# Eight pairs of input tiles of the feed-forward output multiplied by seven block products, three by plain products

## The chip, the cores and the metric

The kernel runs on one core of a Trainium2 chip. The metric is device time in microseconds of one execution, lower is better. Engine names: PE is TensorE (PEld its weight loads), DVE is VectorE, ACT is ScalarE, POOL is GpSimd, SP is SyncE, which here only issues DMAs. ACT issues some DMAs as well.

## The reference

One layer with 1024 tokens and 1024 features. Four mixer branches are gated and merged, then comes a gated feed-forward, then a gated embedding, then a norm. The change is in the second line of the feed-forward; the code of the gates and of the feed-forward input shares a helper with it.

```python
h = rmsnorm(x, g_mix[i])
...
merged = sum(jax.nn.sigmoid(h @ w_merge_gate[i, br]) * (branches[br] @ w_branch[i, br])
             for br in range(N_BRANCH))
x = x + merged @ w_out[i]
h2 = rmsnorm(x, g_ffn[i])
f_gate, f_up = jnp.split(h2 @ w_ffn_in[i], 2, axis=-1)
x = x + (jax.nn.silu(f_gate) * f_up) @ w_ffn_out[i]      # hidden width 2816 = 22 tiles of 128
h3 = rmsnorm(x, g_ple[i])
x = x + jax.nn.sigmoid(h3 @ w_ple_gate[i]) * (p[i].astype(x.dtype) @ w_ple_proj[i])
return rmsnorm(x, g_final)
```

## The kernel before

Features lie on partitions and tokens along the rows, so an activation tile is 128 features by 1024 tokens (512 KB). Every product is computed in three parts to keep the precision of float32: a value is split in a rounded high part (a cast on ACT) and the rest (a subtraction on DVE), the helper `split`, L110 and L111; the matmuls then add high x high, high x low and low x high.

Gates and feed-forward input use `pair` (L537): two output tiles and all eight input tiles at once, as a two by two block product with seven products where eight would be plain. Its weights come in two loads of 512 KB, `ra` and `rb`. `sums` makes the seven weight operands out of them: three are blocks as they come, four are sums or differences on POOL (L548 to L557). `product` splits one such operand and runs 12 matmuls of 128x128 by 512 columns on it. Products 0, 2 and 4 add up in one PSUM bank, `u`, and between them ACT copies its value out (L576 after product 0, L583 after product 2, L588 after product 4); product 2 can't start before the copy after product 0 is done. The seven activation operands (`OPS`) are made once before a stage by `operands`, seven tiles for each of the four pairs of input tiles, 28 tiles in all.

The feed-forward input is 11 steps of two pairs, `fg` (gate half) and `fu` (up half); a step takes its number `j` from its first hidden tile, 0, 2, ... 20. DVE scales and multiplies the blocks (L703 to L709), ACT applies Silu (L706), and ACT's queue stores the two hidden tiles of a step to DRAM in four DMAs of 256 KB (L714).

The feed-forward output, L716 to L767, reads the 22 hidden tiles back (`load_parts`, L167), splits each once and runs plain three-part products in two chunks of hidden tiles, 14 and 8, and two groups of four output tiles. `x2` is the running sum of the layer. After the last chunk `n3.add` makes the next norm's operands (L191, L192) and its sum of squares (L196, L200) of each output tile; in the second group one output tile at a time is finished, so that this work lies beside the products of the next tile. The stage behind it (`pg`, `pq`) needs all eight tiles.

The order of each engine's instructions is fixed when the program is built. Each engine, and each queue that issues DMAs, takes its instructions in that order: what waits keeps everything behind it waiting. Buffers come from pools: 38 of 512 KB for `T`, 8 for `M`, 3 for raw weights `W`, 4 pairs for split weights `WP`. A load into a buffer waits until its last reader is done.

Of the kernel before, what the change touches and what calls it, by code (L numbers as in the profile page):

```python
# [13 lines left out]
P = 128  # L14
# [10 lines left out]
CHUNKS = ((0, 14), (14, 22))  # L25
# [13 lines left out]
def mixers_kernel(ctx, tc, xT, pT, vec, mask, sgu_ln, sgu_wT, sgu_b, w_in, w_tok, w_gate, w_br, w_out,  # L39
                  w_fi, w_fo, w_pg, w_pp, outT):  # L40
# [25 lines left out]
    def M(name, w=S, dt=F32):  # L66
        return mp.tile([P, w], dt, tag="m", name=name, padded_shape=[P, S], bufs=8)
# [4 lines left out]
    def WS(name):  # L72
        return wp.tile([P, 512], F32, tag="sw", name=name, bufs=2)
# [278 lines left out]
    def qk(ct):  # L352

        qs, kd = [], []
        kl = None
        for nm, i in (("q", 6 + ct), ("k", 8 + ct)):
            ps = proj_tile(i)
            t = T(f"{nm}{ct}")
            if nm == "q":
                nc.vector.scalar_tensor_tensor(t, ps, -(64.0 ** -0.5), rs, ALU.mult, ALU.mult)  # L360
                for h in range(2):
                    a, b = slice(h * 64, h * 64 + 64), slice(64 - h * 64, 128 - h * 64)
                    d = M(f"qs{ct}{h}", S, F32R)
                    nc.scalar.copy(d[a, :], t[a, :])
                    nc.vector.tensor_sub(d[b, :], t[a, :], d[a, :].bitcast(F32))
                    qs.append(d)
            else:
                nc.vector.tensor_mul(t, ps, rs)
                kl = M(f"kl{ct}", S, F32R)
                for h in range(2):  # L370
                    a, b = slice(h * 64, h * 64 + 64), slice(64 - h * 64, 128 - h * 64)
                    d = M(f"kd{ct}{h}", S, F32R)
# [60 lines left out]
    sgc = M("sgc", 6 * P).rearrange("p (g c) -> p g c", c=P)  # L433
# [77 lines left out]
    def operand(name, p, i, src):  # L511

        t = T(f"{name}o{p}i{i}", F32R)
        split(t[:, :512], t[:, 512:], src)
        OPS[p][i] = t

    def operands(name, i, xa, xb, have=()):

        a1, a2, b1, b2 = xa[:, :512], xa[:, 512:], xb[:, :512], xb[:, 512:]
        t12, t34 = M(f"{name}t12i{i}"), M(f"{name}t34i{i}")  # L520
        t1, t2, t3, t4 = t12[:, :512], t12[:, 512:], t34[:, :512], t34[:, 512:]
        if 0 not in have:
            operand(name, 0, i, a1)
        nc.vector.tensor_sub(t1, a2, a1)
        operand(name, 1, i, t1)
        nc.vector.tensor_sub(t2, b2, t1)
        operand(name, 2, i, t2)
        if 3 not in have:
            operand(name, 3, i, b1)
        nc.vector.tensor_sub(t3, b2, a2)  # L530
        operand(name, 4, i, t3)
        if 5 not in have:
            operand(name, 5, i, b2)
        nc.vector.tensor_sub(t4, b1, t2)
        operand(name, 6, i, t4)

    def pair(name, wa, wb):  # L537

        ra = W(f"{name}ra")
        nc.sync.dma_start(ra, wa)  # L540
        rb = W(f"{name}rb")
        nc.sync.dma_start(rb, wb)
        a1, a2, b1, b2 = ra[:, :512], ra[:, 512:], rb[:, :512], rb[:, 512:]

        def sums():
            yield a1
# [12 lines left out]
            yield b2

        def product(p, src, ps, first):
            hi, lo = WP(f"{name}p{p}")
            split(hi, lo, src)
            for i in range(4):
                x = OPS[p][i]
                wh, wl = hi[:, i * P:(i + 1) * P], lo[:, i * P:(i + 1) * P]
                for n, (w, c) in enumerate(((wh, 0), (wh, 512), (wl, 0))):
                    nc.tensor.matmul(ps, w, x[:, c:c + 512], start=(first and i == 0 and n == 0),  # L568
                                     stop=(i == 3 and n == 2), skip_group_check=not first)
# [95 lines left out]
    for m0 in (0, 1, 2, 3, 4, 5, 6):  # L665
# [58 lines left out]
    for ci, (k0, k1) in enumerate(CHUNKS):
        fs = {}
        for grp in range(2):
            last = ci == 1 and grp == 1
            if not last:
                ps = [[A(f"fo{ci}{grp}{mm}{h}") for h in range(2)] for mm in range(4)]
                for k in range(k0, k1):  # L730
                    if grp == 0:
                        fs[k] = load_parts(f"f{k}", fd[k])
                    if k % 2 == 0:
                        raw = W(f"fow{grp}{k}")
                        nc.sync.dma_start(raw, w_fo[:, (grp * NJ + k) * 512:(grp * NJ + k + 2) * 512])
                        w = w_parts(f"fow{grp}{k}", raw, S)
                    for mm in range(4):
                        for i, (n, p) in enumerate(((0, 0), (0, 1), (1, 0))):
                            for h in range(2):
                                nc.tensor.matmul(ps[mm][h], w[k % 2 * 4 + mm][n], fs[k].part(p, h * 512, h * 512 + 512),  # L740
                                                 start=(k == k0 and i == 0), stop=(k == k1 - 1 and i == 2))
            if ci == 1 and not last:
                for k in range(2):
                    raw = W(f"pp{k}r")
                    nc.sync.dma_start(raw, pT[k * P:(k + 1) * P, :])
                    pp.append(parts(f"pp{k}", raw))
            for mm in range(4):
                m = 4 * grp + mm
                if last:
                    pm = [A(f"fo{ci}{grp}{mm}{h}") for h in range(2)]  # L750
                    w = []
                    n = (k1 - k0) * P
                    for c in range(0, n, S):
                        e = min(c + S, n)
                        raw = W(f"fol{m}{c}", e - c)
                        nc.sync.dma_start(raw, w_fo[:, (NJ + k0) * 512 + mm * n + c:(NJ + k0) * 512 + mm * n + e])
                        w += w_parts(f"fol{m}{c}", raw, e - c)
                    for k in range(k0, k1):
                        for h in range(2):
                            mm_k(pm[h], w[k - k0], fs[k], k == k0, k == k1 - 1, ((h * 512, h * 512 + 512),), h * 512)  # L760
                else:
                    pm = ps[mm]
                for h in range(2):
                    t = x2[m][:, h * 512:h * 512 + 512]
                    nc.vector.tensor_add(t, pm[h], t)  # L765
                if ci == 1:
                    n3.add(m, x2[m])  # L767
# [101 lines left out]
def _layout(i):  # L869
# [15 lines left out]
    def taps(w):  # L885
# [22 lines left out]
    wo = a["w_ffn_out"][0].reshape(NJ, P, 2, 4, P)  # L908
    k1 = CHUNKS[1][0]
    out["w_fo"] = np.concatenate([t.reshape(P, -1) for t in (  # L910
        wo[:, :, 0].transpose(1, 0, 2, 3), wo[:k1, :, 1].transpose(1, 0, 2, 3), wo[k1:, :, 1].transpose(1, 2, 0, 3))], 1)
# [20 lines left out]
```

## Time and profile before

| | us |
|---|---|
| median of 3 runs (1609.58 to 1611.53) | 1611.34 |
| the profiled execution's own time | 1612.55 |
| its span in the trace | 1610.8 |
| PE busy | 1588.8 (99%) |
| DVE busy | 1031.6 (64%) |
| ACT busy | 640.0 (40%) |
| POOL busy | 215.1 (13%) |
| feed-forward input, steps 2 to 20 (847.7 to 1232.7) | 385.0 |
| feed-forward output (1232.7 to 1472.3) | 239.6 |

Durations are read from the profiled execution, whose own time is 1.21 us above the median. A matmul's record overlaps the next one, so a rate is read from the distance of starts and not from a record's length; the same holds for DVE, where one record of 0.69 us starts 0.60 us after the last.

### The profile page before, as it was taken

Reading aid. Unit: us, or ns where it says so; the run is one execution under the profiler, and the core shown is the slowest. Engines: PE = TensorE matmul, PEld = TensorE weight load, DVE = VectorE, ACT = ScalarE, POOL = GpSimd, SP = SyncE. Lnnn points to the kernel's source line nnn. Section 1 sums busy time; section 2 is a strip of 40 time slices with the busy share of each in tenths; the row PEclk is TensorE's granted clock in tenths of the full one; section 3 lists DMA queues with packets and bytes.
Section 4 is the critical chain, followed back from the end, with each engine's and each line's share of the span. In section 5 each row is a group of like instructions: output and inputs, shape, how many; then the busy total and the mean of one; then the engine's idle time right before and its main releaser. Section 6 shows DMA issues by size and latency. Waiting matters only on the chain.

```text
span 1610.8 us, 19722 instructions
## 1 busy us (share of the span) xinstructions
PE 1588.8 (99%) x7626; PEld 1309.6 (81%) x7626; DVE 1031.6 (64%) x1506; ACT 640.0 (40%) x1068; POOL 215.1 (13%) x158
## 2 busy tenths in 40 slices
PE   9999999999999999999999999999999999999997
PEld 7976788778888888888888888888888888888886
DVE  6988785755567667686776666666666431354456
ACT  6335554233434334354553333433334411133334
POOL 0000000112222222200122322223220000000000
PEclk9999999999999999999999999999999999999998
DMA  6110233121212212213442222222225531211214
GB/s 223 53 40 14 70 129 108 66 79 47 92 53 72 66 52 73 66 59 135 140 176 79 85 79 87 94 82 79 81 89 172 207 92 53 68 41 46 66 47 141
DMA packets 46718, 140.93 MB, mean 87 GB/s; under 512 B 5280, under 2 KB 8608, under 8 KB 46624
## 3 DMA queue, kind: packets, MB, share of 16 engines
q1 hardware_dynamic: 39024, 125.98, 23.8%
q10 hardware_dynamic: 7600, 13.69, 2.3%
q8 instruction: 60, 0.98, 0.3%
q14 instruction: 34, 0.28, 0.1%
HBM read 115.53 MB, written 24.12 MB: 87 GB/s over the span
## 4 chain that ended last, share of the span: by engine, by line
PE 88%; DVE 8%; DMA 1%; ACT 1%; issue 0%; ACTq 0%; SPq 0%; DVEq 0%
PE fo L740 12%; PE pj L151 10%; PE wo L151 5%; PE br L151 5%; PE pg L151 5%; PE fo L151 3%; PE po L413 1%; PE sc L394 1%; PE pq L151 1%; PE ptp L407 1%; PE sc L393 1%; PE sp L317 1%; PE sp L315 1%; PE fu20u L568 1%; PE gt63u L568 1%; PE gt43u L568 1%
## 5 line engine op out<-in xcount | busy, mean ns | idle before, releaser
L330 DVE SCALAR_TENSOR_TENSOR cacc<-cy,vs,cacc 128x1023 f32<-128x1023 f32 (+29 forms) x60 | 75.7, 1263 | 0.5
L408 ACT COPY pt<-ptp 128x512 f32<-128x512 f32 (+3 forms) x48 | 21.8, 481 | 35.5 <-PE ptp L407 35.5
L814 DVE TENSOR_TENSOR pt<-pg,n3r 128x768 f32<-128x768 f32 (+1 forms) x16 | 11.0, 689 | 29.7 <-PE pg L151 29.7
L398 DVE CUSTOM_DVE_ANT_0 pr<-sc,maskt 128x128 f32<-128x128 f32 (+7 forms) x32 | 24.1, 753 | 9.1 <-PE sc L394 8.8
L151 PE MATMUL pj<-n1p,w1h 128*128 128x512 f32 x96 | 27.7, 408 | 1.4 <-ACT n1p L191 1.4
L765 DVE TENSOR_TENSOR x<-fo,x 128x512 f32<-128x512 f32 x32 | 20.9, 687 | 12.5 <-PE fo L151 11.3
L400 ACT ACTIVATE pr<-pr,nm 128x128 f32<-128x128 f32 (+7 forms) x32 | 24.9, 779 | 5.5 <-DVE nm L398 5.3
L438 POOL TENSOR_SCALAR_AFFINE_SELECT sgc<-sgc 128x512 f32<-128x512 f32 x1 | 1.3, 1322 | 168.8 <-DMA sgc<-in_sgu_wT 168.8
L151 PEld LDWEIGHTS pj<-n1p,w1h 128*128 128x128 f32 x96 | 18.7, 196 | 6.2 <-ACT n1p L191 2.2
L413 PE MATMUL po<-pt,vt 128*64 128x128 f32 x288 | 22.7, 279 | 0.2
L407 PE MATMUL ptp<-ident,pr 128*128 128x128 f32 x144 | 22.2, 276 | 0.0
L413 PEld LDWEIGHTS po<-pt,vt 128*64 128x64 f32 x288 | 16.9, 136 | 5.8 <-issue 2.8
L394 PE MATMUL sc<-kl,qs 64*128 64x512 f32 (+3 forms) x48 | 21.0, 438 | 0.0
L815 ACT ACTIVATE pt<-pt 128x768 f32<-128x768 f32 (+1 forms) x16 | 10.1, 630 | 26.3 <-DVE pt L814 26.3
L682 DVE TENSOR_TENSOR xr<-wo,xr 128x512 f32<-128x512 f32 x16 | 11.0, 688 | 14.8 <-PE wo L151 14.7
L407 PEld LDWEIGHTS ptp<-ident,pr 128*128 128x128 f32 x144 | 16.6, 140 | 3.1 <-ACT rb L418 1.0
L393 PE MATMUL sc<-kd,qs 128*128 128x512 f32 (+3 forms) x48 | 18.7, 390 | 0.1
L548 POOL TENSOR_TENSOR gt00s<-gt00rb 128x512 f32<-128x512 f32 x1 | 1.3, 1292 | 131.1 <-DMA gt00rb<-in_w_gate 131.1
L683 ACT ACTIVATE x1g<-xr,vs 128x512 f32<-128x512 f32 x16 | 11.6, 724 | 18.0 <-DVE xr L682 18.0
L394 PEld LDWEIGHTS sc<-kl,qs 64*128 64x128 f32 x48 | 8.8, 183 | 10.0 <-issue 8.6
L822 ACT ACTIVATE pt<-x 128x768 f32<-128x768 f32 (+1 forms) x13 | 8.4, 647 | 19.0 <-DVE x L818 19.0
L151 PE MATMUL pj<-n1p,w1l 128*128 128x512 f32 x48 | 15.3, 398 | 0.0
(4222 smaller groups left out, 5306.7 us busy)
## 6 DMA issues: line engine op xcount, KB each, us to landing
fow<-in_w_fo SPq DMA_DIRECT2D x18, 512.0 KB, 3.8
xg<-in_xT SPq DMA_DIRECT2D x8, 512.0 KB, 4.2
xr<-in_xT SPq DMA_DIRECT2D x8, 512.0 KB, 5.1
x1d<-xr SPq DMA_DIRECT2D x8, 512.0 KB, 2.9
x<-x1d SPq DMA_DIRECT2D x8, 512.0 KB, 5.8
x<-in_xT SPq DMA_DIRECT2D x7, 512.0 KB, 7.5
vpr<-in_w_tok SPq DMA_DIRECT2D x4, 512.0 KB, 4.8
spr<-in_w_tok SPq DMA_DIRECT2D x4, 512.0 KB, 3.6
```

Of the source, the lines that this page charges most:

```text
L151: nc.tensor.matmul(ps[:, c - off:e - off], w[n], act.part(p, c, e), start=(first and i == 0), stop=(last and i == 2))
L330: nc.vector.scalar_tensor_tensor(acc[:, d:], y[:, :S - d], wj, acc[:, d:], ALU.mult, ALU.add)
L393: nc.tensor.matmul(sc[:, c:c + n], q, kd[h][:, c:c + n], start=True, stop=False)
L394: nc.tensor.matmul(sc[:, c:c + n], q[a, :], kl[a, c:c + n], start=False, stop=True)
L398: nc.vector.tensor_tensor_reduce(out=pr[:, :L], in0=sc[:, :L], in1=maskt[:, S - L:], scale=1.0, scalar=NEG, op0=ALU.add, op1=ALU.min, accu ...
L400: nc.scalar.activation(pr[:, :L], pr[:, :L], AF.Exp, bias=nm, scale=-1.0, accum_out=ls)
L407: nc.tensor.transpose(pa[:, j * P:(j + 1) * P], pr[:, c + j * P:c + (j + 1) * P], ident)
L408: nc.scalar.copy(pt[:, c:c + n], pa[:, :n])
L413: nc.tensor.matmul(po[h * 64:h * 64 + 64, :P], vtok[j // 4][:, hc:hc + 64], pts[h][:, j * P:(j + 1) * P], start=(j == 0), stop=(j == b))
L568: nc.tensor.matmul(ps, w, x[:, c:c + 512], start=(first and i == 0 and n == 0), stop=(i == 3 and n == 2), skip_group_check=not first)
L740: nc.tensor.matmul(ps[mm][h], w[k % 2 * 4 + mm][n], fs[k].part(p, h * 512, h * 512 + 512), start=(k == k0 and i == 0), stop=(k == k1 - 1 a ...
L765: nc.vector.tensor_add(t, pm[h], t)
```

## The change

The output of the feed-forward now takes pairs of hidden tiles 0 to 3 and 4 to 7 (two chunks of four pairs, 16 hidden tiles) through `pair`, four pairs of output tiles for each chunk, and hidden pairs 8, 9 and 10 through plain products (`single`). The order is single 8, chunk 0, single 9, chunk 1, single 10. `n3.add` follows each output tile of single 10.

What is stored to DRAM is no longer the hidden tile but the split operands: seven tiles of 512 KB for a pair in a chunk, four for a single one. They are made one step later than their blocks, one after each block of the following step (`next(steps)`), and stored by ACT's queue. The reads back (`load_hidden`) have no split behind them. The operand tiles come from `M`, and so the loads of `x2`, which stood at the start of the feed-forward input, stand at its end: tiles 0 to 3 before the operands of pair 10, tiles 4 to 7 behind them, in the buffers that these four operands had.

The four sums and differences of weights in `pair` run on DVE instead of POOL, in all uses: 16 pairs of the gates, 22 of the feed-forward input, and the 8 new ones.

```diff
-CHUNKS = ((0, 14), (14, 22))
+CHUNKS = ((0, 4), (4, 8))
+SINGLE = (8, 9, 10)
...
         def sums():
             yield a1
-            s1 = WS(f"{name}s1")
-            nc.gpsimd.tensor_add(s1, b1, b2)
+            s1 = WS(f"{name}s1", w)
+            nc.vector.tensor_add(s1, b1, b2)
             yield s1
...
-    fd = []
+    fd = {}
+
+    def store(i, p, t):
+        d = tc.dram_tile([P, S], F32, name=f"fd{p}_{i}")
+        nc.scalar.dma_start(d, t.bitcast(F32))
+        fd[i, p] = d
+
+    def hidden_operands(i, f):
+
+        f = f[0, 0], f[0, 1], f[1, 0], f[1, 1]
+        if i in SINGLE:
+            for p, src in enumerate(f):
+                store(i, p, operand("h", p, i, src, M))
+                yield
+        else:
+            for p, t in operands("h", i, *f, (), M):
+                store(i, p, t)
+                yield
+
+    steps = iter(())
     for j in range(0, NJ, 2):
...
+                next(steps, None)
             both.append(blocks)
-        for k in range(2):
-            d = tc.dram_tile([P, S], F32, name=f"fd{j + k}")
-            for h in range(2):
-                nc.scalar.dma_start(d[:, h * 512:h * 512 + 512], both[0][k, h])
-            fd.append(d)
+        for _ in steps:
+            pass
+        steps = hidden_operands(j // 2, both[0])
...
+    load_x(range(4))
+    for _ in steps:
+        pass
+    load_x(range(4, KD))
...
+    def load_hidden(i, p):
+        t = T(f"hl{p}_{i}", F32R)
+        nc.sync.dma_start(t.bitcast(F32), fd[i, p])
+        return t
+
+    def single_operands(i):
+        t = [load_hidden(i, p) for p in range(4)]
+        return Halves(t[:2]), Halves(t[2:])
+
+    def single(n, acts, done=None):
+        w = []
+        for c in (0, S):
+            raw = W(f"fs{n}{c}")
+            nc.sync.dma_start(raw, w_fs[n, :, c:c + S])
+            w.append(raw)
+        for m in range(KD):
+            if m % 2 == 0:
+                wm = w_parts(f"fs{n}{m}", w[m // 4][:, m % 4 * 256:m % 4 * 256 + 512], 512)
+            for h in range(2):
+                pm = A(f"fs{n}{m}{h}")
+                c = h * 512
+                for k in range(2):
+                    mm_k(pm, wm[m % 2 * 2 + k], acts[k], k == 0, k == 1, ((c, c + 512),), c)
+                x = x2[m][:, c:c + 512]
+                nc.vector.tensor_add(x, pm, x)
+            if done:
+                done(m)
+
+    following = single_operands(SINGLE[0])
+    for ci, (i0, i1) in enumerate(CHUNKS):
+        acts = following
+        for p in range(7):
+            for i in range(4):
+                OPS[p][i] = load_hidden(i0 + i, p)
+        single(ci, acts)
+        following = single_operands(SINGLE[ci + 1])
+        for m in range(0, KD, 2):
+            c = ci * S
+            for k, h, ps, t in pair(f"fo{ci}{m}", w_fo[m, :, c:c + S], w_fo[m + 1, :, c:c + S]):
+                x = x2[m + k][:, h * 512:h * 512 + 512]
+                nc.vector.tensor_add(x, x, t)
+                nc.vector.tensor_add(x, ps, x)
...
+    single(2, following, lambda m: n3.add(m, x2[m]))
```

SP's queue at the end of the feed-forward input, before. `fu20` is the last pair's weights, `fow` the output weights, `f0l` and on the hidden tiles.

```order
L542 DMA fu20rb_9755<-in_w_fi 128x1024
L735 DMA fow00_9933<-in_w_fo 128x1024
L735 DMA fow02_10001<-in_w_fo 128x1024
L167 DMA f0l_9928<-fd0_6938 128x1024
L735 DMA fow04_10069<-in_w_fo 128x1024
```

The same place now. `fs0` is the weights of single 8, `hlP_I` operand P of hidden pair I, `x24` to `x27` tiles 4 to 7 of `x2`, `fo00ra` the first weights of chunk 0.

```order
L760 DMA fs01024_10308<-in_w_fs 128x1024
...
L749 DMA hl1_1_10260<-fd1_1_7385 128x1024
L736 DMA x24_10234<-x1d4_6342 128x1024
L736 DMA x25_10236<-x1d5_6416 128x1024
L749 DMA hl1_2_10262<-fd1_2_7716 128x1024
L736 DMA x26_10238<-x1d6_6589 128x1024
L736 DMA x27_10240<-x1d7_6591 128x1024
L749 DMA hl1_3_10264<-fd1_3_8047 128x1024
L749 DMA hl2_0_10266<-fd2_0_7080 128x1024
...
L749 DMA hl3_9_10460<-fd3_9_10059 128x1024
L537 DMA fo00ra_10462<-in_w_fo 128x1024
```

Before, weights and hidden tiles alternate. Now all 28 operand tiles of chunk 0, four `x2` tiles among them, and the four operands of single 9 stand ahead of chunk 0's first weights.

SP's queue around the last pair of chunk 0 (`fo06`) now; `fs1` is the weights of single 9, `fo10ra` the first weights of chunk 1. There was no such place before.

```order
L539 DMA fo06rb_10887<-in_w_fo 128x1024
L760 DMA fs10_11082<-in_w_fs 128x1024
L760 DMA fs11024_11084<-in_w_fs 128x1024
L749 DMA hl0_4_11026<-fd0_4_8350 128x1024
...
L749 DMA hl6_7_11080<-fd6_7_9564 128x1024
L749 DMA hl0_10_11230<-fd0_10_10217 128x1024
...
L749 DMA hl3_10_11236<-fd3_10_10232 128x1024
L537 DMA fo10ra_11238<-in_w_fo 128x1024
```

28 operand tiles of chunk 1 and four of single 10 stand between the weights of single 9 and those of chunk 1.

ACT's instructions at the start of a step of the feed-forward input (step 8) before, up to the copy that product 2 waits for (L576). `fd` are the stores of the step before.

```order
L714 DMA fd_7826<-fg6n_7540 128x512
L110 CAST fg8p2h<-fg8s_7875 128x512
L714 DMA fd_7829<-fg6n_7540 128x512
L110 CAST fg8p3h<-fg8ra 128x512
L714 DMA fd_7826<-fg6n_7597 128x512
L110 CAST fg8p4h<-fg8s_7915 128x512
L714 DMA fd_7829<-fg6n_7597 128x512
L576 COPY fg8n_7836<-fg8u 128x512
L110 CAST fg8p5h<-fg8s_7875 128x512
```

The same place now; `ho` are the hidden operands, and the copy is L573.

```order
L111 CAST ho0i_8016<-fg6n_7604 128x512
L695 DMA fd_3_8019<-ho0i_8016 128x1024
L111 CAST fg8p2h<-fg8s_7974 128x512
L111 CAST fg8p3h<-fg8ra 128x512
L573 COPY fg8n_7935<-fg8u 128x512
L111 CAST fg8p4h<-fg8s_8021 128x512
L111 CAST ho1i_8044<-ht12i_8014 128x512
```

Before, four stores, each waiting for a product of DVE, stood ahead of the copy. Now one store stands there, three rows ahead of it.

## Rows read from the trace of the kernel before

**Rows 1.** The page, busy us, share of the span and instructions.

```profile
PE 1588.8 (99%) x7626; PEld 1309.6 (81%) x7626; DVE 1031.6 (64%) x1506; ACT 640.0 (40%) x1068; POOL 215.1 (13%) x158
```

**Rows 2.** Stages: start:end, us, busy us (x) by engine, PEclk, DMA share, GB/s.

```profile
330.00:720.00 390.00, 389.05 (x1714) 321.18 (x1713) 257.73 (x375) 160.76 (x268) 87.68 (x60) 1.00 0.21 66
847.70:1232.70 385.00, 383.81 (x1681) 314.58 (x1680) 253.56 (x343) 151.59 (x263) 103.52 (x77) 1.00 0.26 87
1232.70:1472.30 239.60, 239.60 (x1059) 198.40 (x1058) 94.75 (x116) 63.03 (x80) 0.00 (x0) 1.00 0.30 97
```

**Rows 3.** Chain that ended last, in time: start us, us, what; products of step 4.

```profile
890.42 0.70 DVE fg2n L709
891.12 0.02 issue
891.14 0.33 ACTq L714
891.47 0.04 issue
891.51 0.60 ACT fg4n L576
892.11 0.04 issue
892.15 3.02 PE fg4u L568 x12
895.17 2.72 PE fg4c L568 x12
```

**Rows 4.** DVE in time, step 4: start us, us, what.

```profile
898.53 0.68 DVE L111 TENSOR_TENSOR fu4p0l<-fu4ra,fu4p0h 128x512 fp32r<-128x512 f32 x1
899.13 0.69 DVE L704 TENSOR_TENSOR fg4n<-fg4n,n2r 128x512 f32<-128x512 f32 x1
```

**Rows 5.** Stretches of dense loading, columns as in rows 2.

```profile
10.00:15.00 5.00, 5.00 (x23) 4.08 (x22) 4.30 (x6) 5.00 (x8) 0.00 (x0) 1.00 1.04 407
820.00:825.00 5.00, 5.00 (x24) 4.09 (x23) 3.75 (x7) 1.69 (x4) 0.00 (x0) 1.00 0.95 372
1240.00:1290.00 50.00, 50.00 (x222) 41.42 (x221) 24.00 (x24) 19.51 (x23) 0.00 (x0) 1.00 0.56 199
```

**Rows 6.** The page, DMA queue and issues: MB and share; KB each, us to landing.

```profile
q1 hardware_dynamic: 39024, 125.98, 23.8%
...
fow<-in_w_fo SPq DMA_DIRECT2D x18, 512.0 KB, 3.8
...
x1d<-xr SPq DMA_DIRECT2D x8, 512.0 KB, 2.9
```

**Rows 7.** Around the end of the feed-forward output, columns as in rows 2.

```profile
1479.20:1485.40 6.20, 6.20 (x22) 5.34 (x23) 3.24 (x6) 0.67 (x2) 0.00 (x0) 0.54 0.00 0
1485.40:1489.60 4.20, 4.20 (x24) 3.49 (x22) 0.00 (x0) 1.23 (x3) 0.00 (x0) 1.00 0.37 125
```

**Rows 8.** The chain there, columns as in rows 3.

```profile
1475.60 1.23 DVE n3sq L200
1476.83 0.04 issue
1476.87 2.46 PE n3ss L210 x16
1479.33 6.22 PE pg L151 x20
...
1490.89 8.59 PE pg L151 x48
```

**Rows 9.** DVE groups of that stretch: shapes, count, busy us, mean ns.

```profile
L765 DVE TENSOR_TENSOR x<-fo,x 128x512 f32<-128x512 f32 x32 | 20.9, 687 | 12.5 <-PE fo L151 11.3 <-PE fo L740 0.7
L192 DVE SCALAR_TENSOR_TENSOR n3l<-x,vs,n3h 128x1024 fp32r<-128x1024 f32 x8 | 10.3, 1282 | 2.5 <-ACT n3h L191 2.5
L200 DVE TENSOR_TENSOR n3sq<-n3sq,n3sq 128x1024 f32<-128x1024 f32 x7 | 8.5, 1219 | 0.0
```

More of the change, by code (lines that the diff above doesn't have):

```diff
@@ L39, in mixers_kernel @@
 def mixers_kernel(ctx, tc, xT, pT, vec, mask, sgu_ln, sgu_wT, sgu_b, w_in, w_tok, w_gate, w_br, w_out,
-                  w_fi, w_fo, w_pg, w_pp, outT):
+                  w_fi, w_fo, w_fs, w_pg, w_pp, outT):
     nc = tc.nc
@@ L64, in T, with M @@
         return op.tile([P, w], dt, tag="o", name=name, padded_shape=[P, S], bufs=38)
-    def M(name, w=S, dt=F32):
+    def M(name, dt=F32, w=S):
         return mp.tile([P, w], dt, tag="m", name=name, padded_shape=[P, S], bufs=8)
@@ L70, in W, with WS @@
         return wp.tile([P, w], F32, tag="wr", name=name, padded_shape=[P, S], bufs=3)
-    def WS(name):
-        return wp.tile([P, 512], F32, tag="sw", name=name, bufs=2)
+    def WS(name, w=512):
+        return wp.tile([P, w], F32, tag="sw", name=name, padded_shape=[P, 512], bufs=2)
     def WP(name):
@@ L362, in qk @@
                     a, b = slice(h * 64, h * 64 + 64), slice(64 - h * 64, 128 - h * 64)
-                    d = M(f"qs{ct}{h}", S, F32R)
+                    d = M(f"qs{ct}{h}", F32R)
                     nc.scalar.copy(d[a, :], t[a, :])
@@ L368, in qk @@
                 nc.vector.tensor_mul(t, ps, rs)
-                kl = M(f"kl{ct}", S, F32R)
+                kl = M(f"kl{ct}", F32R)
                 for h in range(2):
                     a, b = slice(h * 64, h * 64 + 64), slice(64 - h * 64, 128 - h * 64)
-                    d = M(f"kd{ct}{h}", S, F32R)
+                    d = M(f"kd{ct}{h}", F32R)
                     nc.scalar.copy(d[a, :], t[a, :])
@@ L509, in mixers_kernel, with operand, operands @@
     OPS = [[None] * 4 for _ in range(7)]
-    def operand(name, p, i, src):
-        t = T(f"{name}o{p}i{i}", F32R)
+    def operand(name, p, i, src, alloc=T):
+        t = alloc(f"{name}o{p}i{i}", F32R)
         split(t[:, :512], t[:, 512:], src)
-        OPS[p][i] = t
-    def operands(name, i, xa, xb, have=()):
-        a1, a2, b1, b2 = xa[:, :512], xa[:, 512:], xb[:, :512], xb[:, 512:]
+        return t
+    def operands(name, i, a1, a2, b1, b2, have=(), alloc=T):
         t12, t34 = M(f"{name}t12i{i}"), M(f"{name}t34i{i}")
@@ L521, in operands @@
         t1, t2, t3, t4 = t12[:, :512], t12[:, 512:], t34[:, :512], t34[:, 512:]
[L522 to L534, printed above, removed]
@@ L535, in operands, with keep_operands @@
-        operand(name, 6, i, t4)
-    def pair(name, wa, wb):
-        ra = W(f"{name}ra")
+        for p, (src, sub) in enumerate(((a1, None), (t1, (a2, a1)), (t2, (b2, t1)), (b1, None), (t3, (b2, a2)),
+                                        (b2, None), (t4, (b1, t2)))):
+            if sub:
+                nc.vector.tensor_sub(src, *sub)
+            if p not in have:
+                yield p, operand(name, p, i, src, alloc)
+    def keep_operands(name, i, xa, xb, have=()):
+        for p, t in operands(name, i, xa[:, :512], xa[:, 512:], xb[:, :512], xb[:, 512:], have):
+            OPS[p][i] = t
@@ L540, in pair @@
+    def pair(name, wa, wb, n=4):
+        w = n * P
+        ra = W(f"{name}ra", 2 * w)
         nc.sync.dma_start(ra, wa)
-        rb = W(f"{name}rb")
+        rb = W(f"{name}rb", 2 * w)
         nc.sync.dma_start(rb, wb)
-        a1, a2, b1, b2 = ra[:, :512], ra[:, 512:], rb[:, :512], rb[:, 512:]
+        a1, a2, b1, b2 = ra[:, :w], ra[:, w:], rb[:, :w], rb[:, w:]
         def sums():
             yield a1
-            s1 = WS(f"{name}s1")
-            nc.gpsimd.tensor_add(s1, b1, b2)
+            s1 = WS(f"{name}s1", w)
+            nc.vector.tensor_add(s1, b1, b2)
@@ L549, in sums @@
             yield s1
-            s2 = WS(f"{name}s2")
-            nc.gpsimd.tensor_sub(s2, s1, a1)
+            s2 = WS(f"{name}s2", w)
+            nc.vector.tensor_sub(s2, s1, a1)
             yield s2
             yield a2
-            s3 = WS(f"{name}s3")
-            nc.gpsimd.tensor_sub(s3, a1, b1)
+            s3 = WS(f"{name}s3", w)
+            nc.vector.tensor_sub(s3, a1, b1)
             yield s3
-            nc.gpsimd.tensor_sub(s2, a2, s2)
+            nc.vector.tensor_sub(s2, a2, s2)
@@ L562, in product @@
             hi, lo = WP(f"{name}p{p}")
-            split(hi, lo, src)
-            for i in range(4):
+            split(hi[:, :w], lo[:, :w], src)
+            for i in range(n):
                 x = OPS[p][i]
                 wh, wl = hi[:, i * P:(i + 1) * P], lo[:, i * P:(i + 1) * P]
-                for n, (w, c) in enumerate(((wh, 0), (wh, 512), (wl, 0))):
-                    nc.tensor.matmul(ps, w, x[:, c:c + 512], start=(first and i == 0 and n == 0),
-                                     stop=(i == 3 and n == 2), skip_group_check=not first)
+                for j, (ww, c) in enumerate(((wh, 0), (wh, 512), (wl, 0))):
+                    nc.tensor.matmul(ps, ww, x[:, c:c + 512], start=(first and i == 0 and j == 0),
+                                     stop=(i == n - 1 and j == 2), skip_group_check=not first)
         src = sums()
@@ L709, in mixers_kernel @@
                     nc.vector.tensor_mul(g, g, t)
+                next(steps, None)
             both.append(blocks)
-        for k in range(2):
-            d = tc.dram_tile([P, S], F32, name=f"fd{j + k}")
-            for h in range(2):
-                nc.scalar.dma_start(d[:, h * 512:h * 512 + 512], both[0][k, h])
-            fd.append(d)
-    x2 = []
-    for m in range(KD):
-        x2.append(M(f"x2{m}"))
-        nc.sync.dma_start(x2[m], x1d[m])
+        for _ in steps:
+            pass
@@ L722, in mixers_kernel, with load_x @@
+        steps = hidden_operands(j // 2, both[0])
+    x2 = []
+    def load_x(ms):
+        for m in ms:
+            x2.append(M(f"x2{m}"))
+            nc.sync.dma_start(x2[m], x1d[m])
+    load_x(range(4))
+    for _ in steps:
+        pass
+    load_x(range(4, KD))
     n3 = Norm("n3", V_GPLE, False)
     pp = []
[L724 to L742, printed above, removed]
-                for k in range(2):
[L744 to L767, printed above, removed]
@@ L768, in mixers_kernel @@
+    for k in range(2):
+        raw = W(f"pp{k}r")
+        nc.sync.dma_start(raw, pT[k * P:(k + 1) * P, :])
+        pp.append(parts(f"pp{k}", raw))
+    single(2, following, lambda m: n3.add(m, x2[m]))
     banks.close()
@@ L907, in _layout @@
     out["w_fi"] = halves(tiles(a["w_ffn_in"][0]))
[L908 to L911, printed above, removed]
+    wo = tiles(a["w_ffn_out"][0])
+    out["w_fo"] = np.concatenate([halves(wo[:, :, i * 2 * P:j * 2 * P]) for i, j in CHUNKS], 2)
+    out["w_fs"] = np.stack([wo[:, :, i * 2 * P:(i + 1) * 2 * P].transpose(1, 0, 2).reshape(P, 2 * S) for i in SINGLE])
     out["w_pg"] = tiles(a["w_ple_gate"][0])
```

7 lines of the change are left out of this document (4 added, 3 removed).

## The prediction

> **What bounds the kernel now.** I read the busy times first. PE is busy 99% of the span, so time goes where PE's work or PE's waits go [rows 1]. Then I cut the span by stage. In the feed-forward output PE is busy 239.60 of 239.60 us. In the feed-forward input it lacks 1.19 of 385.00 us, and in the gates 0.95 of 390.00. DVE is at 66% in the last two [rows 2]. The chain of waits then gives the size of a product: 2.72 us for 12 matmuls, 0.2267 us each [rows 3]. Last come the densest stretches of loading, because the change loads much more [rows 5, 6], and the end of the output stage, where PE does wait [rows 7, 8].
>
> **PE's own work.** Before, the output stage is 22 x 8 x 3 x 2 = 1056 matmuls. Now the eight pairs are 2 chunks x 4 output pairs x 7 products x 12 = 672, and the three single ones 3 x 8 x 12 = 288, together 960. That is 96 x 0.2267 = **-21.8 us**. Same shape of matmul, so nothing is uncertain in this term.
>
> **The feed-forward input.** Product 2 waits for ACT's copy after product 0. In the trace that copy starts 0.04 us after a store that waited for DVE's product, and product 2 shows 3.02 us instead of 2.72 [rows 3]. Ten steps took 385.00 us [rows 2] where 10 x 14 x 2.72 = 380.8 would do, so 0.42 us a step. In the new order of ACT only one store stands in that stretch, and what it waits for is done some 5.6 us before the copy is due. I take **-4.2 us** (0 to -4.2). The price is more work on DVE. A step had 34 DVE instructions and has 53: eight sums, seven operand splits and four differences more. DVE instructions start 0.60 us apart [rows 4], so 53 x 0.61 = 32.3 us in 38.1 us of PE. ACT gets seven casts more; each store now waits there for DVE's half of its split, one after another, and behind it wait casts of weights that are needed two or more products (5.4 us) later. The free time of both hides this at nothing; without it each microsecond a step is late costs 10 us. In the gates the 64 sums are 39 us more DVE in 390, so 297 of 390, also hidden, 0 (-1 to 1).
>
> **Loads ahead of chunk 0.** This is the largest term. Let 0 be the start of `fu20`'s product 0, the last pair of the feed-forward input. It ends at 7 x 2.72 = 19.0, single 8 at 19.0 + 96 x 0.2267 = 40.8, and there PE wants chunk 0's first weights.
> SP's queue reaches `fs01024` at about 1.6, once DVE has split product 3's weights, and then has ten operand tiles whose buffers are free. Then comes `x24`. It takes the `M` buffer of pair 10's operand 0, so it waits until that operand is made and stored. ACT's cast of that operand stands behind a cast that needs product 4 to be over (13.6) and behind the copy after product 4, so it ends at 15.4; DVE's half at 16.1; the store takes 2.9 us to land [rows 6]: `x24` goes at about 20. Operand 1 stands behind a cast that waits for product 6 (19.0) and five DVE instructions: stored at 22.2, `x25` at 25.2. Operands 2 and 3 need the last block and stand behind the first adds of single 8: stored at 25.4 and 26.0, `x26` at 28.3 and `x27` at 29.
> From about 29.5 on, 27 loads of 512 KB stand in order: `x27`, 21 operand tiles, four of single 9, and `fo00ra`. In dense stretches the engines moved 372 GB/s at a share of 0.95 (392 when full), 407 at 1.04, 199 at 0.56 (355) [rows 5]; the whole of queue 1 gives 125.98 MB / (0.238 x 1610.8 us) = 329 [rows 6]. I take 360 GB/s, near the row of output weights, so 1.46 us a tile, with 1.29 (407) and 1.59 (329) as bounds. The first lands after 3.8 us [rows 6], the 27th after 26 x 1.46 more, and the cast is 0.6: 29.5 + 3.8 + 38.0 + 0.6 = 71.9. PE waits 71.9 - 40.8 = **31.1 us** (26.6 to 34.4). Without the hold at `x24` it would be 41 more tiles from 1.6 on, 65.9, still 25.1: the volume makes the wait, the hold adds six.
> The Trainium skill, page DMA: Bandwidth & Descriptors, section Bandwidth, has a 16 MB load on one core at 425 GB/s; no stretch of this trace reaches it. At that rate a tile would take 1.23 us, this wait be 25.2 and the next 6.0, and the total some 1629.
>
> **Loads ahead of chunk 1.** The 28 buffers come free as chunk 0's last pair, `fo06`, goes through its products, 2.72 us for four tiles, faster than the 5.84 us that four take to load, so loading binds. SP gets past `fs11024` 1.6 us into `fo06`; PE wants `fo10ra` 40.8 us into it, after single 9. It is the 34th load: 1.6 + 3.8 + 33 x 1.46 + 0.6 = 54.2, a wait of **13.4 us** (7.8 to 17.7).
>
> **The end of the stage.** Before, only the last output tile's `n3.add` came after the products: from PE's last product (1472.3) to the sum of squares' matmuls (1476.87) are 4.6 us [rows 2, 8]. In single 10 a tile takes PE 2.72 us, and DVE two adds, a split and a sum: 2 x 0.65 + 1.25 + 1.2 = 3.75, by the records of that stretch less their overlap [rows 9]. For eight tiles, with two weight splits: 16 x 0.65 + 8 x 1.25 + 7 x 1.2 + 2 x 0.6 = 30.0, begun 1.6 us after the first product and with 1 us of waits: 32.6, where PE is done at 21.8. So 10.9 us instead of 4.6, **+6.3**, and 0.6 for three or four matmuls more behind the sum in PE's order: **+6.9** (5 to 9).
>
> **The clock.** After PE's gap and its 16 tiny matmuls there, the granted clock is 0.54 for 6.2 us, about 1.2 GHz, with 22 matmuls; the next 4.2 us at 1.00 hold 24 [rows 7]. At that pace 22 take 3.85 us, so one such fall costs 2.4. I take one after each of the two waits, **+4.8** (0 to 6).
>
> **Sum.** -21.8 - 4.2 + 31.1 + 13.4 + 6.9 + 4.8 = +30.2 on the profiled execution's 1612.55, so 1642.8. The median is 1.21 lower: **1641.5, forecast 1642**. With every lower bound, but full relief in the input stage: -26.0 + 26.6 + 7.8 + 5 = +13.4, 1625. With every upper bound: -21.8 + 34.4 + 17.7 + 9 + 6 + 1 = +46, 1657.
>
> **Rivals.**
> *The loads come in time: not slower.* Place: SP's two bursts. No stretch before has thirty tiles queued, so the full rate may never have shown; against it speaks that the share already reads 0.95 to 1.04. Without both waits and without clock falls the sum is -21.8 - 4.2 + 6.9 = -19.1, so 1592. With one clock fall left, the two waits must shrink from 44.5 to 16.7 for no change: at 0.9 us a tile (580 GB/s) the second is gone and the first is 29.5 + 4.4 + 26 x 0.9 - 40.8 = 16.5. No row comes near that rate. Chance 0.11, of which 0.04 near no change.
> *DVE becomes the bound of the feed-forward input: slower still.* For it: 32.3 of 38.1 us in a fixed order, and the first sum of a pair stops DVE until `rb` has landed, where it stopped only POOL. Against: by the order, at 0.60 us an instruction, SP asks for the next `rb` some 5.6 us into a pair, it lands 3.8 later, and the split behind that sum is due at product 6, at 16.3. At 3 us a step it is +30 instead of -4: 1642 + 34 = 1676. Chance 0.05.
> *The bursts and the tail are both milder than any bound*: between no change and 1622, say 1618. Chance 0.04.
>
> **How the numbers follow.** Forecast 0.80, with its bounds widened by 3 us below (the first pairs of a stage, where `rb` is late): 1622 to 1657. That is the range; 0.15 lies below it, 0.05 above. A run tells this kernel from no change at about 0.2%, 3.2 us. Faster: 0.07 of the first rival. Same: 0.04. Slower: 0.80 + 0.05 + 0.04 = 0.89.
>
> **What would show it.** In the new profile: 960 matmuls in the output stage at 0.227 us; `fg` product 2 without its extra 0.3 us; PE idle for about 31 us before `fo00u`, ended by ACT's cast of `fo00ra` or its load, and about 13 us before `fo10u`; SP waiting at the loads of `x2`'s tiles 4 to 7; DMA shares near 1 in both gaps; a granted clock near 0.5 behind each; and some 11 us from single 10's last matmul to `n3ss`. The forecast is wrong if the gap before `fo00u` is under 15 us, or if a step of the feed-forward input is over 39 us.

## The result and the profile after

The changed kernel took 1634.76 us, the median of four runs (1634.07 to 1636.87), against 1611.43 for the kernel before (four runs, 1609.58 to 1611.96): a ratio of 1.0149, 95% interval 1.0131 to 1.0167. A second set of runs gave 1634.23 and 1.0146 (1.0132 to 1.0159). It is slower by 23.3 us, inside the predicted range (1622 to 1657) and 7 us under the forecast of 1642.

The page of the changed kernel, busy us, share of the span and instructions, and of its DMA part packets, MB and share, KB each and us to landing:

```profile
PE 1568.4 (96%) x7530; PEld 1295.0 (79%) x7530; DVE 1184.0 (73%) x1872; ACT 683.7 (42%) x1170; POOL 1.9 (0%) x6
...
q1 hardware_dynamic: 45648, 150.10, 26.9%
...
hl<-fd SPq DMA_DIRECT2D x68, 512.0 KB, 10.2
```

Against [rows 1], PE has 96 matmuls fewer and is busy 20.4 us less, yet its share fell from 99% to 96%: the time is in waits. Queue 1 moves 24 MB more than in [rows 6], and a 512 KB load now lands 10.2 us after it is asked for, where such a load of weights took 3.8.

The stages of the changed kernel, columns as in [rows 2]:

```profile
330.00:720.00 390.00, 389.01 (x1714) 321.13 (x1713) 280.89 (x435) 161.23 (x269) 0.00 (x0) 1.00 0.21 65
847.20:1228.00 380.80, 380.80 (x1682) 315.31 (x1681) 318.28 (x516) 182.83 (x325) 0.00 (x0) 1.00 0.45 161
1249.80:1278.70 28.90, 0.10 (x1) 0.00 (x0) 0.69 (x1) 0.62 (x1) 0.00 (x0) 0.55 1.03 410
1278.70:1283.90 5.20, 5.18 (x13) 4.07 (x14) 5.12 (x8) 1.76 (x3) 0.00 (x0) 0.56 0.14 57
1378.90:1388.50 9.60, 0.20 (x1) 0.00 (x0) 0.71 (x2) 0.62 (x1) 0.00 (x0) 0.68 0.97 387
1488.50:1498.50 10.00, 3.54 (x19) 2.58 (x17) 9.98 (x12) 6.91 (x8) 0.00 (x0) 0.99 0.00 1
```

The first two rows answer to [rows 2]: the gates are unchanged (389.01 of 390 us busy, 389.05 before), and ten steps of the feed-forward input, the same 1681 matmuls or so, fill 380.80 us without a gap where they took 385.00. In the third row PE stands for 28.9 us while the DMA engines are at a share of 1.03, in the fifth for 9.6 us. In the fourth, behind the wait, the granted clock is 0.56, near the lower of its two levels (1.2 GHz). In the last, the end of the stage, DVE works 9.98 of 10.00 us and almost nothing is loaded.

What ended PE's waits there (engine, tile, line, what it waited for, us in total, times, longest):

```profile
PE fo00u L565 <- ACT fo00p0h L111: 28.8, 1, 28.8
PE fo10u L565 <- ACT fo10p0h L111: 9.4, 1, 9.4
PE n3ss L211 <- DVE n3sq L201: 5.0, 1, 5.0
```

The chain that leads to the first wait, in order of time, columns as in [rows 3]:

```profile
1230.25 3.73 DMA x<-x1d
1233.98 0.69 DVE ho3i L112
1234.70 4.13 DMA fd<-ho3i
...
1239.79 7.46 DMA hl<-fd
...
1257.56 10.18 DMA hl<-fd
1267.75 10.22 DMA fo00ra<-in_w_fo
...
1278.05 0.63 ACT fo00p0h L111
...
1278.72 5.14 PE fo00u L565 x12
...
1388.51 4.88 PE fo10u L565 x12
...
1497.28 1.23 DVE n3sq L201
1498.55 3.57 PE n3ss L211 x16
...
1513.09 8.59 PE pg L152 x48
```

Read backwards from `fo00u`: the product waits for ACT's cast, the cast for `fo00ra`, and `fo00ra` was asked for only at 1267.75, behind the operand tiles. Before them, loads and stores of `x2` and pair 10 come. The product itself then takes 5.14 us, not 2.72, and the first product of chunk 1, behind the second wait, 4.88. The last rows are the end of the stage: the last sum of squares, its matmuls (`n3ss`), and the first 48 matmuls of `pg01`. What stood in SP's queue (start us, us, what, count):

```profile
1212.10 9.54 SPq L749 DMA_DIRECT2D hl<-fd  x10
1230.25 5.36 SPq L736 DMA_DIRECT2D x<-x1d  x2
1235.70 1.04 SPq L749 DMA_DIRECT2D hl<-fd  x1
1236.85 2.36 SPq L736 DMA_DIRECT2D x<-x1d  x2
1239.30 27.48 SPq L749 DMA_DIRECT2D hl<-fd  x25
1267.75 0.33 SPq L537 DMA_DIRECT2D fo00ra<-in_w_fo  x1
```

Ten tiles, then a halt of 8.6 us at `x24`, then 25 more tiles ahead of the first weights, 1.27 us from one issue to the next at the end.

### The profile page after: what moved, and what is told of

It is laid out like the page before. It is cut to its first block, busy times and chain, and to the rows that moved or that the text cites. A ratio compares the mean times of both kernels' runs of the same rounds, so it can differ in the third digit from the quotient of the medians.

```text
span 1632.3 us, 19841 instructions
## 1 busy us (share of the span) xinstructions
PE 1568.4 (96%) x7530; PEld 1295.0 (79%) x7530; DVE 1184.0 (73%) x1872; ACT 683.7 (42%) x1170; POOL 1.9 (0%) x6
## 4 chain that ended last, share of the span: by engine, by line
PE 89%; DMA 6%; DVE 4%; issue 1%; ACT 1%; SPq 0%; DVEq 0%; ACTq 0%
PE pj L152 10%; PE wo L152 5%; PE br L152 5%; PE pg L152 5%; DMA hl<-fd 3%; PE po L414 1%; PE pq L152 1%; PE sc L395 1%; PE ptp L408 1%; PE sc L394 1%; PE fo00u L565 1%; PE fo10u L565 1%; DMA fo00ra<-in_w_fo 1%; DMA fo10ra<-in_w_fo 1%; PE sp L318 1%
## 5 line engine op out<-in xcount | busy, mean ns | idle before, releaser
L771 DVE TENSOR_TENSOR x<-fs,x 128x512 f32<-128x512 f32 x48 | 32.2, 688 | 18.7 <-PE fs L152 18.5
L409 ACT COPY pt<-ptp 128x512 f32<-128x512 f32 (+3 forms) x48 | 21.8, 480 | 35.5 <-PE ptp L408 35.5
L565 PE MATMUL fo00u<-hl,fo00p0h 128*128 128x512 f32 x8 | 4.2, 630 | 28.8 <-ACT fo00p0h L111 28.8
L841 ACT ACTIVATE pt<-pt 128x768 f32<-128x768 f32 (+1 forms) x16 | 10.1, 631 | 26.3 <-DVE pt L840 26.3
## 6 DMA issues: line engine op xcount, KB each, us to landing
hl<-fd SPq DMA_DIRECT2D x68, 512.0 KB, 10.2
```

The source lines that it names most:

```text
L409: nc.scalar.copy(pt[:, c:c + n], pa[:, :n])
L565: nc.tensor.matmul(ps, ww, x[:, c:c + 512], start=(first and i == 0 and j == 0), stop=(i == n - 1 and j == 2), skip_group_check=not first)
L771: nc.vector.tensor_add(x, pm, x)
```

## The experiments

Two things differ between the profiled executions by about 2 us each, whatever the edit: where `fu20` starts (1207.9 to 1210.5 us) and the pace of the last stage (e10). So beside a total stands the time from the start of `fu20` to `n3ss`, 289.6 us in the changed kernel (1208.94 to 1498.55), which holds neither.

**x2's tiles 4 to 7 on their own queue (e1).**

```diff
-            nc.sync.dma_start(x2[m], x1d[m])
+            (nc.gpsimd if m >= 4 else nc.sync).dma_start(x2[m], x1d[m])
```

> Theory (order in SP's queue): the loads of x2's tiles 4 to 7 hold SP, and all loads behind them, while pair 10's operands are stored; on the idle POOL queue they hold nobody. SP then asks for 36 operand tiles and fo00ra without a stop from 10 us before the end of fu20's product 4 on; with the four x2 tiles these are 41 tiles of 512 KB at 1.28 us, so fo00ra lands some 18 us after PE wants it instead of 28.8: total about 1624. The wait before fo10u stays at 9.5. The prediction's own figure for the hold, six us, would give 1629. Rival (the volume at a rate that products beside it lower): the tiles come no earlier, the wait stays near 28 us and the total near 1634.

1633.72 us; `fu20` to `n3ss` 286.7 us (2.9 less), the wait before `fo00u` 26.3 (2.5 less). SP no longer stops, but `fo00ra` is asked for 53.2 us after the first operand tile (1213.61 to 1266.77), hardly sooner than the 55.7 of the changed kernel. The same two stretches, from the tenth tile's issue to that of `x24` and from there to that of `x27`, first in the changed kernel and then, at the same distance from `fu20`'s start, in this one:

```profile
1221.60:1230.20 8.60, 8.60 (x39) 7.13 (x38) 8.04 (x14) 3.49 (x6) 0.00 (x0) 1.00 0.89 355
1230.20:1239.30 9.10, 9.10 (x41) 7.51 (x41) 7.29 (x13) 1.15 (x2) 0.00 (x0) 1.00 0.80 266
```

```profile
1223.10:1231.70 8.60, 8.60 (x40) 7.12 (x39) 8.04 (x14) 3.49 (x6) 0.00 (x0) 1.00 1.02 392
1231.70:1240.80 9.10, 9.10 (x42) 7.54 (x41) 7.29 (x13) 1.14 (x2) 1.22 (x2) 1.00 1.02 398
```

While SP stood, the engines still had the ten tiles and pair 10's stores to move and ran at shares of 0.89 and 0.80. Only what is missing to 1.02 is lost, some 3 us. All three expectations missed: 18 us (theory), 6 us less (the prediction) and no change (rival). The rival's number is nearest, but its reason isn't: beside PE's products the engines moved 392 and 398 GB/s, hardly less than the 410 of the wait. My count left out traffic: from the first issue to `fo00ra`'s landing the engines move 24.8 MB (9.5, 8.6, 9.1 and 36.1 us at 340, 392, 398 and 405 GB/s), 47 tiles of 512 KB, not 41. Pair 10's four stores are among them; the rest, not traced one by one, would be what was in flight at either end.

**The first weights of a chunk on their own queue (e2).**

```diff
+        q = nc.gpsimd if name in ("fo00", "fo10") else nc.sync
         ra = W(f"{name}ra", 2 * w)
-        nc.sync.dma_start(ra, wa)
+        q.dma_start(ra, wa)
         rb = W(f"{name}rb", 2 * w)
-        nc.sync.dma_start(rb, wb)
+        q.dma_start(rb, wb)
```

> Only the weights of each chunk's first pair go to the idle POOL queue, so they stand behind no operand tile; the same bytes are loaded. Theory (order): the wait before fo00u goes; what is left is that the last operand tiles of chunk 0 land about 1275 and product 6 of fo00 wants them at 1266, so some 7 to 9 us of waits in front of products 4 to 6; the wait before fo10u is gone; the granted clock falls less: total about 1600 (1597 to 1605). Rival (volume): the first pair of a chunk waits for operand tiles as long as it waited for weights, and the total stays within 5 us of 1634.

1609.21 us, ratio to the kernel before 0.9986 (0.9977 to 0.9996); `fu20` to `n3ss` 262.1 us, 27.5 less. What is left of PE's waits in the stage is in these rows (as above):

```profile
PE fo00e L566 <- DMA hl<-fd: 10.6, 1, 10.6
PE n3ss L211 <- DVE n3sq L201: 5.0, 1, 5.0
...
PE fo00c L566 <- DMA hl<-fd: 0.6, 2, 0.3
PE fo10e L566 <- ACT fo10p6h L111: 0.5, 1, 0.5
```

The same bytes, and 38.2 us of waits became 11.7. So most of both waits was order. The rest is volume: product 6 (`fo00e`) waits for its own operand tiles, the last four of the 28. It comes to 10.6 instead of 7 to 9 because the new order on PE puts product 6 ahead of products 2, 4 and 5, whose tiles are there sooner, and the clock falls behind that wait too (`fo00e` takes 4.71 us). The total misses my 1600 by 9: the waits by 3 to 5 us, the clock by 2, and some 2 from the last stage (from `n3ss` to the end 135.9 us for 133.75).

**The sums back on POOL (e3).**

```diff
-            nc.vector.tensor_add(s1, b1, b2)
+            nc.gpsimd.tensor_add(s1, b1, b2)
...
-            nc.vector.tensor_sub(s2, a2, s2)
+            nc.gpsimd.tensor_sub(s2, a2, s2)
```

> Only the four sums of weights a pair go back from DVE to POOL. Theory: they are hidden on either engine, and the 0.42 us a step that the feed-forward input lost before came from the stores in ACT's order: the input stage stays at 380.8 us, the total at 1635 (1633 to 1638). Rival: the 0.42 us came from POOL's sums, so fg's product 2 waits again, the input stage goes back to 385 and the total to 1639.

1637.33 us. The input stage, columns as in [rows 2]:

```profile
847.20:1228.00 380.80, 380.80 (x1681) 315.31 (x1680) 312.85 (x438) 183.31 (x324) 115.81 (x77) 1.00 0.44 162
```

PE has no gap there with the sums on POOL, so they weren't what cost 0.42 us a step. `fu20` to `n3ss` is 290.6, 1 us more (the wait before `fo00u` 30.4); the rest of the 2.6 us lies in the two unsteady places. Outside them, moving the sums was worth about 1 us.

**The last single product ahead of the last pair (e4).**

```diff
+            if (ci, m) == (1, 6):
+                single(2, following, lambda m: m < 6 and n3.add(m, x2[m]))
...
-    single(2, following, lambda m: n3.add(m, x2[m]))
+    for m in (6, 7):
+        n3.add(m, x2[m])
```

> Single 10 is computed before the last pair of chunk 1 instead of after it, so that six of the eight n3.add stand beside products. Theory (DVE's work behind the last products makes the tail): from PE's last product to n3ss about 4.6 us instead of 10.0, and to pg01 18.6 instead of 24.6: total about 1629. Rival (what follows the sum of squares, not DVE, sets the time of pg01): the total stays at 1634 or 1635.

1630.16 us, 4.6 less where I expected 6. PE's waits:

```profile
PE fo16u L565 <- ACT fo16n L573: 1.9, 1, 1.9
PE n3ss L211 <- DVE n3sq L201: 1.2, 1, 1.2
```

The wait for the sum of squares falls from 5.0 to 1.2, so DVE's work behind the last products did make the tail. From PE's last product to `n3ss` it is 5.6 us and to `pg01` 15.9, where I expected 4.6 and 18.6: the granted clock stays at 1.00 behind `n3ss` here, where it was 0.61 from 1498.55 to 1507.0 in the changed kernel. But a new wait of 1.9 us stands before a product of `fo16`, since ACT's casts and squares of `n3.add` are now ahead of its copies, and the clock falls behind it (0.61 over the next 4.4 us). So `pg01` comes 5.8 us sooner after `fu20`; the last stage ran at its slower pace (e10) and took some of that back. The theory holds; that the total came near my 6 is in part two misses that cancel.

**The next single's operands after the first pair (e5).**

```diff
-        following = single_operands(SINGLE[ci + 1])
         for m in range(0, KD, 2):
+            if m == 2:
+                following = single_operands(SINGLE[ci + 1])
```

> Only the four operand tiles of the next single product are asked for after a chunk's first pair instead of ahead of it, in both chunks. Theory (each tile that stands ahead of a chunk's first weights in SP's queue costs 1.28 us of PE's wait): the wait before fo00u falls by 5.1 to 23.7 us, that before fo10u by 5.1 to 4.4: total about 1624.5. Rival (the first weights wait for something else, a free buffer of theirs): both waits and the total stay.

1627.37 us; `fu20` to `n3ss` 279.7, 9.9 less. The waits:

```profile
PE fo00u L565 <- ACT fo00p0h L111: 23.2, 1, 23.2
...
PE fo10u L565 <- ACT fo10p0h L111: 4.5, 1, 4.5
```

Four tiles less ahead of the weights: 5.6 and 4.9 us less, 1.2 to 1.4 a tile, as expected. Each tile there is paid in full. The total misses the expected 1624.5 by 2.9 us, in the two unsteady places: `fu20` starts 1.2 us later, and from `n3ss` to the end it is 135.5 us for 133.75.

**The kernel before with its hidden tiles stored from SP (e6).**

```diff
-                nc.scalar.dma_start(d[:, h * 512:h * 512 + 512], both[0][k, h])
+                nc.sync.dma_start(d[:, h * 512:h * 512 + 512], both[0][k, h])
```

> The kernel before, with nothing changed but the queue of the stores of the hidden tiles in the feed-forward input: SP instead of ACT. Theory (such a store, waiting in ACT's order for DVE's product, delays ACT's copy and by it product 2 of fg): the input stage falls from 385.0 to about 381 us and the total by 4.2 to about 1607.5. Rival: the copy waits for something else, and the input stage stays at 385, the total at 1612. Second rival: a store that waits on SP delays the weights' loads behind it and the stage grows.

1606.49 us, ratio 0.9974 (0.9963 to 0.9984). Its input stage and, from the chain, the product that took 3.02 us in [rows 3]:

```profile
848.50:1229.30 380.80, 380.80 (x1682) 315.32 (x1681) 258.32 (x342) 150.90 (x262) 103.12 (x77) 1.00 0.26 88
```

```profile
892.05 2.72 PE fg4u L568 x12
```

No gap is left, and the kernel before gains 4.8 us by one word. Together with e3 this settles the term: the stores in ACT's order made the 0.42 us a step.

**Time to load: two singles ahead of chunk 0 (e7).**

```diff
-    following = single_operands(SINGLE[0])
...
-        acts = following
+        singles = ((0, 1), (2,))[ci]
+        acts = [single_operands(SINGLE[n]) for n in singles]
...
-        single(ci, acts)
-        following = single_operands(SINGLE[ci + 1])
+        for n, a in zip(singles, acts):
+            single(n, a)
...
+            for k in range(2 * ci):
+                n3.add(m + k, x2[m + k])
...
-    single(2, following, lambda m: n3.add(m, x2[m]))
```

It has e2's edit as well, and loads single 9's weights on POOL's queue.

> Singles 8 and 9 ahead of chunk 0, single 10 ahead of chunk 1, n3.add of two output tiles after each pair of chunk 1; the weights of single 9 and of each chunk's first pair on the POOL queue. Theory (order and the time there is to load): chunk 0's last operand tile lands some 73 us after fu20's start, where product 6 of fo00 wants it at 79, so neither chunk waits, the granted clock stays at 1.00, and the tail shrinks by 5: 1634.8 - 28.8 - 9.4 - 4.6 - 5 = 1587 (1585 to 1593). Rival (volume, as it was left in the run with the weights on their own queue): some 10 us of waits for the last operand tiles stay, total about 1600.

1594.91 us, ratio 0.9896 (0.9881 to 0.9911); `fu20` to `n3ss` 245.0. PE's waits from `fu20` to the gates of the last stage:

```profile
PE pq L152 <- ACT pp0h L111: 5.3, 1, 5.3
...
PE fo00e L566 <- ACT fo00p6h L111: 0.5, 1, 0.5
PE fo10e L566 <- ACT fo10p6h L111: 0.5, 1, 0.5
```

Both waits are gone with more tiles ahead of chunk 0 than ever, since PE wants them 21.8 us later. The total lies outside the expected range, 8 us over the 1587. The largest part is a new wait of 5.3 us, for the casts of `pp`, which stand on ACT behind the last `n3.add`: with it the tail from PE's last product to `pg01` is 23.5 us, 1 less than the 24.6 where I expected 5 less. The two waits of 0.5 add 1 us. The profiled execution was the fastest of the four (1592.76); the 2 us between it and the median aren't explained.

**`pp` loaded and split before pair 2 of chunk 1 (e8).** Against e7:

```diff
         for m in range(0, KD, 2):
+            if (ci, m) == (1, 2):
+                for k in range(2):
+                    raw = W(f"pp{k}r")
+                    nc.sync.dma_start(raw, pT[k * P:(k + 1) * P, :])
+                    pp.append(parts(f"pp{k}", raw))
...
-    for k in range(2):
-        raw = W(f"pp{k}r")
-        nc.sync.dma_start(raw, pT[k * P:(k + 1) * P, :])
-        pp.append(parts(f"pp{k}", raw))
```

> As the run with two singles first, but pp's two tiles are loaded and split before pair 2 of chunk 1 instead of after the last pair. Theory (in that run the tail was set by buffers: pp's casts stood on ACT behind the last n3.add, and PE waited 5.3 us for pp0h): that wait goes, what is late next is the sum of squares for n3ss, some 2 us sooner than pp0h was: total 3 to 4 us less than 1594.9, about 1591. Rival (the first gate matmuls wait for the sum of squares anyway and pq only fills that wait): no change, 1595.

1606.75 us: a miss, 12 us worse than e7. The chain of waits, columns as in [rows 3]:

```profile
1395.92 1.23 DVE pp0l L112
...
1397.16 3.98 DMA fo12rb<-in_w_fo
...
1401.89 0.63 ACT fo12p1h L111
...
1402.56 5.46 PE fo12q L566 x12
```

`pp`'s raw tiles keep two of the three weight buffers until DVE has split them, `fo12rb` waits for one, and PE waits 8.4 us for `fo12p1h`, with the clock down behind it. I had looked at ACT's order only.

**`pp` between the last pair and the last two `n3.add` (e9).** Against e7, with the same lines taken out after the loop:

```diff
+            if (ci, m) == (1, 6):
+                for k in range(2):
+                    raw = W(f"pp{k}r")
+                    nc.sync.dma_start(raw, pT[k * P:(k + 1) * P, :])
+                    pp.append(parts(f"pp{k}", raw))
             for k in range(2 * ci):
                 n3.add(m + k, x2[m + k])
```

> As the run with two singles first, but pp's two tiles are loaded and split after the last pair's products and ahead of the last two n3.add; the weights' buffers are then free. Theory (in that run pp's casts stood on ACT behind the last n3.add, and PE waited 5.3 us for pp0h): the wait goes and n3ss comes some 3 us sooner: total about 1591 (1589 to 1594). Rival (the sum of squares is no earlier, since pp's two casts and splits now stand ahead of it on ACT and DVE): the sum of squares takes over the wait, total 1595 as it was.

1585.53 us (1584.06 to 1590.13), ratio 0.9844 (0.9829 to 0.9860): faster than both kernels, by 26 and 49 us, and 3 under the expected range. Against the kernel before with e6's edit it is 21 us, close to the 21.8 of PE's own work. The profiled execution took 1590.13, the longest of the five, and lies in the range; its stretch from `fu20`'s product 0 to some 2 us before the end of the output stage's last product, columns as in [rows 2], and PE's waits there and for `n3ss`:

```profile
1209.90:1447.10 237.20, 236.24 (x1038) 193.92 (x1037) 165.07 (x252) 81.03 (x132) 3.33 (x6) 1.00 0.59 225
```

```profile
PE n3ss L211 <- DVE n3sq L201: 1.0, 1, 1.0
PE fo10e L566 <- ACT fo10p6h L111: 0.5, 1, 0.5
PE fo00e L566 <- ACT fo00p6h L111: 0.5, 1, 0.5
```

PE is busy for all but 1 of 237 us, and the granted clock is 1.00 throughout: with the waits its falls are gone from this stretch. The wait for `pp0h` is gone as expected, but not by an earlier sum of squares: from `fu20` to `n3ss` it is 244.4 us, only 0.6 less than in e7, where I expected 3. PE now does the products of `pp` and the first of `pg` ahead of `n3ss` instead of behind it, and `pg01` comes some 4.5 us sooner. That accounts for the expected 1591. Why three of the five executions took about 1585 and two 1590 stays open.

**The changed kernel again (e10).** No edit.

> The changed kernel as it is, once more. In most runs of its variants 48 matmuls of the last stage took 8.48 us, in its own profile and in the kernel before 8.32, with the same instructions there. If that goes with the run or the chip, it may read 8.48 here and the total 1637; if it goes with the program (where its buffers lie), it reads 8.32 again and the total is 1634.8 within 1.

1634.23 us; the profiled execution took 1636.44, the other three 1633.70 to 1634.45. A group of 48 matmuls of the last stage in the chain, first in the changed kernel's first profile, then in this one:

```profile
1523.76 8.32 PE pg L152 x48
```

```profile
1535.30 8.48 PE pg L152 x48
```

The same program shows both paces, so the program, and with it where its buffers lie, doesn't set the pace. Nor does the chip alone: e5 (8.48) and e7 (8.32) ran on one chip. Over the stage it is some 1.6 us: from `n3ss` to the end of the span 135.4 us here and 133.75 in the first profile. My total of 1637 for the slower pace holds for the profiled execution, not for the median.

## Why the prediction was right

Term by term, on the profiled executions:

| term | predicted | measured |
|---|---|---|
| PE's own work | -21.8 | 96 matmuls less of 0.2267 us: -21.8 |
| feed-forward input | -4.2 | 385.00 to 380.80: -4.2 |
| wait before `fo00u` | +31.1 | +28.8 |
| wait before `fo10u` | +13.4 | +9.4 |
| tail to `pg01` | +6.9 | 24.6 for 18.6 us: +6.0 |
| clock behind the two waits | +4.8 | 5.14 and 4.88 for 2.72 us: +4.6 |
| sum | +30.2 | +22.8; spans +21.5, medians +23.3 |

The forecast of 1642 was 7 us too high; five of the six terms have the size they were given within 2.5 us, and the second wait is 4 short.

- **Direction and mechanism: shown.** Waits ended by ACT's cast of the first weights, loads in order ahead of them (e2, e5), a clock fall behind each, and room for the waits to go when the order and the time to load change (e7, e9).
- **The mis-sized term is the rate of loading.** I took 360 GB/s and 1.46 us a tile; the stretch of the wait moved 410 at a share of 1.03, 1.28 us a tile, at my bound from the 407 row of [rows 5]. The one load that counts still lands late, because about eight are in flight (10.2 us to landing at 1.28 a tile) and share the engines: from `x27`'s issue (1238.89) to `fo00ra`'s landing (1277.97) 39.1 us passed, 41.8 by my sum. For the second wait it was 47.7 (1340.04 to 1387.7) for 52.0. The Trainium skill, page DMA: Bandwidth & Descriptors, section Bandwidth, gives 425 GB/s for a 16 MB load; the measured 410 lies nearer to that than to my 360, and the estimate from it, some 1629 (its terms add up to 1628), lay about as far below the result as mine lay above.
- **The hold at `x24`: wrong in size.** "The hold adds six" was 2.5 to 2.9 (e1). I let the engines stand while SP stood, and left out pair 10's stores. The 31.1 doesn't rest on the six: it counts from `x27`, which went 29.95 us after `fu20`'s start for the 29.5 I took, so that only the rate shows in it. My 25.1 without the hold came near e1's 26.3 by luck: 41 tiles at 1.46 us are 59.9 us, and what the engines moved was 47 at 1.28, 60.2.
- **Feed-forward input: right, and for the reason given** (e3, e6). DVE did not become the bound: it is busy 318 of 381 us, and PE does not wait. In the gates it is busy 281 of 390 us, where I had worked out 297, and PE is as busy there as before.
- **The tail: right.** 10.0 us from PE's last product to `n3ss` for the 10.9 worked out, and DVE's adds, splits and sums behind the last products are what fills it (e4).
- **The rivals.** The loads did not come in time: the row of 410 GB/s is far from the 580 that would have made no change.

## What to carry to other kernels

Where PE has no slack, work out when the bytes of a stage can be there: buffers' release, then tiles by 1.28 us each here, up to the load that PE wants first. What it wants first must not stand in an in-order queue behind what it wants last, and small independent products are worth most where they buy loading time (e7: 21.8 us more of PE work ahead of a chunk, on top of e2's edit, brought what was left of its wait from 10.6 to 0.5 us). A stopped queue cost here only what the DMA engines stood idle (e1), and a move that looks right in one engine's order can still take a buffer that another load needs (e8).

## What the runs showed of the hardware

- One core's loads of 512 KB held 410 GB/s at a share of 1.03 for 28.9 us, 10.2 us from issue to landing and 1.27 us from one issue to the next, so with about eight in flight on SP's queue.
- With two of `x2`'s tiles on POOL's queue beside SP's loads the rate did not rise: 398 GB/s at a share of 1.02 in e1's row.
- The matmuls of the last stage run at one of two paces, 8.32 or 8.48 us for 48, at the same granted clock of 1.00 and in the same program. What sets it stays open.
